# Running sums of the exponentials on two engines, pinned lane work, and value products of two key blocks in a row, in a conformer and attention layer

## The chip, the cores and the metric

The kernel runs on one core of a Trainium2 chip. Its engines are TensorE (PE in the profile, with its weight loads as PEld), VectorE (DVE), ScalarE (ACT), GpSimd (POOL) and SyncE (SP, which issues most DMAs). The metric is the device time of one execution in microseconds, the median of several runs. Before the change it is 2803.77 us, from three runs between 2798.85 and 2807.2.

## The reference, cut to what matters

One layer of a streaming encoder for a prompt of 2048 frames and, beside it, 8 sample streams of 16 new frames with 1024 cached ones each. Half of the channels go through a convolution module, half through attention with a forget bias; one output projection and a feed-forward network follow.

```python
def _conv_module(u_hist, conv_w, conv_b, ln_g, ln_b):
    y = lax.conv_general_dilated(...) + conv_b
    mu = jnp.mean(y32, axis=-1, keepdims=True)
    var = jnp.mean(jnp.square(y32 - mu), axis=-1, keepdims=True)
    y32 = (y32 - mu) * lax.rsqrt(var + EPS) * ln_g + ln_b
    return jax.nn.silu(y32)

def _attend(q, k, v, cum_q, cum_k, q_pos, k_pos):
    s = jnp.einsum('bqhd,bkhd->bhqk', q, k) * (HEAD_DIM ** -0.5)
    s = s + (cum_q[..., :, None] - cum_k[..., None, :])
    s = jnp.where(k_pos[None, :] <= q_pos[:, None], s, NEG_INF)
    p = jax.nn.softmax(s, axis=-1)
    return jnp.einsum('bhqk,bkhd->bqhd', p, v)
...
    mix = jnp.concatenate([conv_out, attn_out], axis=-1) @ w_out
    x = x + g1 * mix
    h = _rmsnorm(x, norm2_g) * (1 + sc2) + sh2
    x = x + g2 * ((silu(h @ w_gate) * (h @ w_up)) @ w_down)
```

There are 8 heads of 64 channels. The softmax divides by the sum of the exponentials, and it is these sums that the change adds up in another way.

## The kernel before

The stages follow one another: modulation and projections (to about 620 us), attention (621 to 1177), the output projection (`project_out`, from 1187), and the two halves of the feed-forward network. All of it is fp32, so that most products run in two passes and show as two records in the profile. The change touches the attention stage.

`attend` runs one of 16 steps: a pair of heads p (0 to 3) and a block of 512 queries qb (0 to 3). It goes over 4 qb + 4 key blocks of 128; the last four lie on the diagonal and are cut and masked. For each key block and head, PE makes the scores in two products (L1004 and L1010, with a mask at L1012) in one of three PSUM banks, ACT the exponential e (L1014). `values` (L971) then multiplies e with V, in tiles of 64 columns, one for each head, side by side; it is called two key blocks behind the scores. The sums of the exponentials are made on PE too, by products with ones (`add_up`, L960) in tiles of 32 columns, up to four of them side by side. For full key blocks GpSimd first adds the exponentials of two neighbouring blocks (tile `two`, L980), so that PE has 96 terms of full blocks; the blocks on the diagonal go to PE one by one (128 terms). At the end of a step the sums are stored, inverted (L1058) and read back some scores later by a list of due times, and the values divided (L1066).

Other work is woven into the steps. `score_maxima` computes an upper bound of the scores ahead of them: a product (mx, L923) in one of two banks, reduced on DVE (M, L928); it runs 32 scores and more ahead. `background` is the "lane": it holds one PSUM bank and runs five chunks of `conv_norm` (the layer norm of the convolution) and eight `sample_batch` (attention of the sample streams) one after another. Each is a generator that gives way at its `yield`s; `nback` is the number of such parts that the steps share out. Lane instructions get a later priority (`BACK_BY`) when they are issued. `behind` pins a product of the lane behind the newest score product, but most of the lane's operations on DVE, ACT and PE are not pinned, so the scheduler places them where their data is ready. A sample batch makes scores with cached keys (kc) and with its new ones (kS), adds them to a tile S, takes the maximum, the exponential, transposes S, multiplies with cached values (vc) and new ones (vn), scales the result (ob) and transposes it into catS.

`project_out` accumulates in all eight PSUM banks, and its eighth is the lane's, so its products for that bank stand behind the lane's end. Its first 63 products fill seven banks.

Of the kernel before, what the change touches and what calls it, by code (L numbers as in the profile page):

```python
# [16 lines left out]
P = 128  # L17
# [101 lines left out]
class Layer:  # L119
# [587 lines left out]
    def conv_norm(self, ch, sp, bank):  # L707
# [9 lines left out]
        def channel_mean(src):  # L717
            pm = bank
            for j in range(4):
                self.behind(nc.tensor.matmul)(pm[32 * j:32 * j + 32, :n], self.ones[:, 0:32], src[j], start=True, stop=True,  # L720
                                 tile_position=(0, 32 * j))
            m = sp.tile([P, 512], F32, tag="cm", name="cm")
            nc.scalar.copy(m[:, :n], pm[:, :n])
            po = bank
            nc.tensor.matmul(po[:, :n], self.mean, m[:, :n], start=True, stop=True)
            return po

        mu = channel_mean([y[:, j, :n] for j in range(4)])
        ms = sp.tile([P, 512], F32, tag="cw", name="cmu")
        nc.scalar.copy(ms[:, :n], mu[:, :n])  # L730
        yield
        sqs = []
        for j in range(4):
            nc.vector.tensor_tensor(y[:, j, :n], y[:, j, :n], ms[:, :n], ALU.subtract)
            sq = sp.tile([P, 512], F32, tag="cq", name="cq", bufs=4)
            nc.scalar.activation(sq[:, :n], y[:, j, :n], AF.Square)
            sqs.append(sq[:, :n])
        yield
        var = channel_mean(sqs)
        v = sp.tile([P, 512], F32, tag="cv", name="cvar")[:, :n]  # L740
        nc.vector.tensor_scalar(v, var[:, :n], EPS, None, ALU.add)
        r = sp.tile([P, 512], F32, tag="cr", name="cr")[:, :n]
        nc.scalar.activation(r, v, AF.Ln)
        nc.scalar.activation(r, r, AF.Exp, scale=-0.5)
        newton_rsqrt(nc, r, sp.tile([P, 512], F32, tag="cm", name="ct")[:, :n], v, 1)
        yield
        for j in range(4):
            z = y[:, j, :n]
            nc.vector.tensor_tensor(z, z, r, ALU.mult)
# [30 lines left out]
    def attention(self, ctx):  # L780
# [4 lines left out]
        self.waiting, self.due, self.last_s = [], [], None  # L785
# [11 lines left out]
        nback, done, units, scored = 15 + 5 * 9 + 12 + 8 * 11, 0, 0, AHEAD  # L797
# [37 lines left out]
    def first_weights(self):  # L835
# [109 lines left out]
    def attend(self, p, qb, n):  # L945
# [5 lines left out]
        z, sums = [], []  # L951

        started = set()

        def add_up(terms, last=False):
            if terms and not started:
                z.append(self.bank("tr", "sm"))
# [7 lines left out]
        def values(kt, off, es):  # L965
# [4 lines left out]
            for h in range(2):  # L970
                product = nc.tensor.matmul(z[0][HD * h:HD * h + HD, off:], V[kt // 4][:, kt % 4, HD * h:HD * h + HD], es[h][:, off:],  # L971
                                           start=(kt == 0), stop=(kt == nkt - 1), tile_position=(0, HD * h))
                if h == 0:
                    self.after(product, self.last_s)
            self.last_product = product
            if kt < 4 * qb:
                if kt % 2 == 0:
                    for h in range(2):
                        two = wk.tile([P, 512], F32, tag="two", name="two", bufs=6)
                        nc.gpsimd.tensor_tensor(two, es[h], self.waiting[0][3][h], ALU.add)  # L980
# [6 lines left out]
            if kt % 2 == 0:  # L987
                return
            if kt == nkt - 1:
                zc = wk.tile([P, 512], F32, tag="zc", name="zc")  # L990
                self.last_exp = nc.scalar.copy(zc, z[0])  # L991
            add_up(sums, kt == nkt - 1)
            sums.clear()
            if kt == nkt - 1:
                self.end_of_step(p, qb, zc, z[1])

        for kt in range(nkt):
# [4 lines left out]
            for h in range(2):  # L1002
# [10 lines left out]
                e = wk.tile([P, 512], F32, tag="e", name="e", bufs=12)  # L1013
                self.last_piece = nc.scalar.activation(e[:, off:], s[:, off:], AF.Exp)  # L1014
# [16 lines left out]
    def end_of_step(self, p, qb, zc, sums):  # L1031
# [37 lines left out]
        self.due += [(self.nscore + k, f) for k, f in ((2, load), (6, invert), (9, back), (14, divide))]  # L1069

    def behind(self, op):

        def issue(*args, **kw):
            ins = op(*args, **kw)
            self.after(ins, self.last_s)
            return ins
        return issue

    def sample_setup(self, bank):
# [27 lines left out]
        for kt in range(8):  # L1107
            self.behind(nc.tensor.matmul)(pt[:n, 2 * kt:2 * kt + 2], lf[:, kt, :], self.ones[:, 0:2], start=True, stop=True)
        suf = sm.tile([P, 8], F32, name="suf")
        nc.vector.memset(suf[:n, 7:8], 0.0)  # L1110
        for kt in range(6, -1, -1):
            nc.vector.tensor_tensor(suf[:n, kt:kt + 1], pt[:n, 2 * kt + 2:2 * kt + 3], suf[:n, kt + 1:kt + 2], ALU.add)
        yield
        for b in range(2):
            pb = bank.rearrange("p (i k) -> p i k", i=4)
            for i in range(4):
                self.behind(nc.tensor.matmul)(pb[:n, i, :], lf[:, 4 * b + i, :], tri, start=True, stop=True)
            nc.vector.tensor_tensor(
                bias[:n, b * 512:(b + 1) * 512].rearrange("p (i k) -> p i k", i=4), pb[:n],
# [7 lines left out]
        nc.tensor.matmul(pn[:n, :], lm.rearrange("p s h -> p (s h)"), sel[:, NS:], start=True, stop=True)  # L1127
# [25 lines left out]
    def sample_batch(self, b, bank):  # L1153
# [4 lines left out]
        for c in range(3):  # L1158
# [8 lines left out]
            pc = bank  # L1167
            for g in range(NP):
                self.behind(nc.tensor.matmul)(pc[32 * g:32 * g + 32, :w], self.Qbd[:, g, b].rearrange("p h q -> p (h q)"), kt[:, g, :],
                                              start=True, stop=True, tile_position=(0, 32 * g))  # L1170
# [4 lines left out]
            nc.vector.tensor_tensor(S[:, c0:c0 + w], S[:, c0:c0 + w], pc[:, :w], ALU.add)  # L1175
            if c == 2:
                nc.vector.tensor_tensor(S[:, c0:], S[:, c0:], self.maskS, ALU.add)
            yield
        nm = sm.tile([P, 1], F32, tag="nm", name="nm", bufs=2)
# [586 lines left out]
```

## Time and profile before

| | |
|---|---|
| Median of three runs | 2803.77 us |
| The profiled execution's own time | 2804.06 us |
| Its span in the profile | 2802.3 us |
| Mean granted PE clock | 0.985 |
| Attention, first score to last sum | 621.4 to 1176.4 us |
| First product of project_out | 1187.18 us |
| First product in the lane's bank | 1205.05 us |

In the profile a group of instructions is named by its line, engine and tiles, followed by its count, its busy time and the mean of one in ns, and by the idle time of its engine just ahead of it with what ended it. A busy time of PE holds everything between issue and end of its matmuls, pipeline fill included. A row of waits gives the total, the number and the longest of one. In a timeline the first column is the start in us, the second the duration of a row; neighbours of one kind share a row, with their count. PE's weight loads run beside its products.

### The profile page before, as it was taken

The page shows a single profiled execution, that of the slowest core. Times are in us where ns is not written, and L with a number is a line of the kernel's source. Part 1 is how long each engine was busy: PE and PEld are TensorE (multiplying, and loading weights), DVE is VectorE, ACT ScalarE, POOL GpSimd, SP SyncE. Part 2 cuts the span into 40 slices and gives each one's busy share as a digit, 9 for nine tenths or more (in the row PEclk, how much of TensorE's full clock was granted, in tenths as well). Part 3 has the DMA queues.
Part 4 walks back from the last instruction along what each step waited for, and adds up shares of the span by engine and source line. Part 5 has one row for each costly group of instructions (what it writes and reads, how often), then busy time and mean ns, then how long its engine had stood idle before and what let it go on. Part 6 is the DMA issues. An engine that isn't in the chain of part 4 may idle for free. (4 is left out here: it accounts for less than half of the span.)

```text
span 2802.3 us, 48143 instructions
## 1 busy us (share of the span) xinstructions
PE 2719.9 (97%) x16666; PEld 2388.6 (85%) x16666; DVE 1975.1 (70%) x3951; ACT 1237.1 (44%) x2406; POOL 461.2 (16%) x616
## 2 busy tenths in 40 slices
PE   7999999999999999999999999999999999999999
PEld 6899988864445545499999999999999999999999
DVE  2798898966465454235397989877886778766765
ACT  4443323344343444434354446444554446555552
POOL 3454411222222222214201121000000000000000
PEclk9999999989999999999999999999999999999999
DMA  9753567674426676355576869866786769788873
GB/s 328 248 192 107 189 220 265 203 199 123 124 73 192 175 233 176 116 192 187 177 265 205 305 204 314 272 217 214 240 288 208 227 194 319 245 279 262 274 252 116
DMA packets 406348, 603.49 MB, mean 215 GB/s; under 512 B 61556, under 2 KB 264468, under 8 KB 404056
## 3 DMA queue, kind: packets, MB, share of 16 engines
q1 hardware_dynamic: 405976, 600.31, 66.7%
q8 instruction: 131, 2.15, 0.3%
q14 instruction: 113, 0.93, 0.1%
q0 software_dynamic: 128, 0.11, 0.0%
HBM read 426.00 MB, written 174.25 MB: 214 GB/s over the span
## 5 line engine op out<-in xcount | busy, mean ns | idle before, releaser
L1556 PE MATMUL z<-rT,rW 128*128 128x360 f32 (+1 forms) x8316 | 1383.7, 328 | 4.5 <-ACT rW L1260 1.4
L1556 PEld LDWEIGHTS z<-rT,rW 128*128 128x128 f32 x8316 | 1379.8, 188 | 6.3 <-ACT rW L1260 2.1
L1260 ACT ACTIVATE rW<-rR 128x512 fp32r<-128x512 f32 x714 | 434.1, 616 | 382.5 <-PE z L1556 275.9
L1261 DVE TENSOR_TENSOR rW<-rR,rW 128x512 fp32r<-128x512 f32 x714 | 476.8, 673 | 149.3 <-ACT rW L1260 144.7
L702 DVE SCALAR_TENSOR_TENSOR cv<-cu,cpar,cv 128x384 f32<-128x384 f32 x580 | 311.7, 615 | 2.9 <-ACT cv L700 2.9
L928 DVE TENSOR_REDUCE M<-mx 128x1 f32<-128x512 f32 (+2 forms) x320 | 189.7, 607 | 146.5 <-PE mx L923 105.2
L1014 ACT ACTIVATE e<-s 128x512 f32<-128x512 f32 (+3 forms) x320 | 168.4, 533 | 278.2 <-PE s L1012 140.2
L514 PE MATMUL z<-hqx,wqh 128*128 128x384 f32 (+1 forms) x768 | 197.5, 333 | 0.1
L980 POOL TENSOR_TENSOR two<-e 128x512 f32<-128x512 f32 x96 | 127.2, 1342 | 398.3 <-ACT e L1014 328.0
L1260 ACT ACTIVATE rT<-traw 128x360 fp32r<-128x360 f32 (+1 forms) x315 | 149.3, 501 | 91.7 <-DMA traw<-gt_d 58.1
L1261 DVE TENSOR_TENSOR rT<-traw,rT 128x360 fp32r<-128x360 f32 (+1 forms) x315 | 157.7, 531 | 42.7 <-ACT rT L1260 42.4
L923 PEld LDWEIGHTS mx<-K,Q 96*128 96x128 f32 x320 | 63.7, 201 | 116.6 <-DVE M L928 54.7
L923 PE MATMUL mx<-K,Q 96*128 96x512 f32 (+2 forms) x320 | 145.2, 463 | 17.1 <-DVE M L928 12.6
L971 PE MATMUL pv<-e,V 128*64 128x512 f32 (+3 forms) x640 | 156.6, 565 | 3.0 <-ACT zc L991 3.0
L514 PEld LDWEIGHTS z<-hqx,wqh 128*128 128x128 f32 x768 | 136.0, 188 | 16.6 <-issue 12.4
L1484 DVE TENSOR_TENSOR rR<-rR 128x512 f32<-128x512 f32 (+1 forms) x136 | 94.2, 712 | 57.2 <-DMA rR<-w_down 52.0
L1244 PE MATMUL acc<-ch,woh 128*128 128x360 f32 (+1 forms) x384 | 128.1, 336 | 4.9 <-DVE xo L1252 2.6
L1244 PE MATMUL acc<-ch,wol 128*128 128x360 f32 (+1 forms) x384 | 128.1, 334 | 0.0
L1004 PE MATMUL s<-Q,K 128*128 128x512 f32 (+3 forms) x320 | 127.6, 399 | 0.0
L514 PE MATMUL z<-hqx,wql 128*128 128x384 f32 (+1 forms) x384 | 126.5, 329 | 0.0
L1244 PE MATMUL acc<-cl,woh 128*128 128x360 f32 (+1 forms) x384 | 122.3, 331 | 0.0
L1010 PE MATMUL s<-Q,K 128*128 128x512 f32 (+3 forms) x320 | 119.3, 373 | 0.0
(307 smaller groups left out, 3581.5 us busy)
## 6 DMA issues: line engine op xcount, KB each, us to landing
rR<-sup_d SPq DMA_DIRECT2D x176, 256.0 KB
rR<-w_gate SPq DMA_DIRECT2D x132, 256.0 KB
traw<-gt_d SPq DMA_DIRECT2D x154, 180.0 KB
rR<-w_down SPq DMA_DIRECT2D x104, 256.0 KB
rR<-sdn_d SPq DMA_DIRECT2D x96, 256.0 KB
rR<-w_up SPq DMA_DIRECT2D x88, 256.0 KB
sup_d<-rR SPq DMA_DIRECT2D x88, 256.0 KB
wa<-w_ada SPq DMA_DIRECT2D x16, 1024.0 KB
```

The costliest lines, as they stand in the source:

```text
L514: nc.tensor.matmul(z[:, :n], w[:, m], x[:, :n], start=(c == 0 and k == 0), stop=(c == CB - 1 and k == 2))
L702: self.pin(nc.vector.scalar_tensor_tensor(dst, src, w, acc[i], ALU.mult, ALU.add))
L923: self.mx.append(nc.tensor.matmul(mx[:, :w], Q2[0:AUX, h, j * P:(j + 1) * P], K2[kb][0:AUX, h, :w], start=True, stop=not diag))
L928: self.last_max = nc.vector.tensor_reduce(M[:, i, kb:kb + 1], mx[:, :w], AX.X, ALU.max)
L971: product = nc.tensor.matmul(z[0][HD * h:HD * h + HD, off:], V[kt // 4][:, kt % 4, HD * h:HD * h + HD], es[h][:, off:], start=(kt == 0), s ...
L980: nc.gpsimd.tensor_tensor(two, es[h], self.waiting[0][3][h], ALU.add)
L1004: first = nc.tensor.matmul(s[:, off:], K1[kb][:, h, sl], Q1[:, h, off:], start=True, stop=False)
L1014: self.last_piece = nc.scalar.activation(e[:, off:], s[:, off:], AF.Exp)
L1244: self.nc.tensor.matmul(z[:, :n], w[:, m], y, start=(first and i == 0 and k == 0), stop=(last and i == len(terms) - 1 and k == 2))
L1260: copy = self.nc.scalar.activation(hi, raw, AF.Copy)
L1261: engine.tensor_tensor(lo, raw, f32(hi), ALU.subtract)
L1556: nc.tensor.matmul(z, W[:, x, m], t[:, y, :w], start=(k == 0 and i == 0), stop=(k == n - 1 and i == 2))
```

## The change

Three things change in the attention stage.

- **Sums.** For the full key blocks of a step, one running sum for each head is kept in SBUF: GpSimd adds the first head's exponentials, DVE the second's, 84 adds each in all. At the diagonal the running sums are multiplied with ones together with the diagonal's terms. PE's terms of full blocks fall from 96 to 24; the 128 of the diagonal stay and are dealt out otherwise among the four tiles.
- **Values.** `values` is called for two key blocks in a row, at every odd key block, when more than three wait. The products of the second are pinned behind those of the first. There are 16 buffers for e, 12 before.
- **Lane.** All operations of the lane are pinned behind the newest operation of attention on their engine: behind the last score on PE, the last exponential on ACT, the last reduce on DVE, the last running sum on GpSimd. The lane is cut into more parts (237, not 160). The 40 subtractions and multiplications of `conv_norm` move from DVE to GpSimd. vn is loaded earlier. The due times of the division grow, and w_out's raw tiles share a ring of four buffers with the running sums.

The core of the diff:

```diff
@@ conv_norm
-            nc.vector.tensor_tensor(y[:, j, :n], y[:, j, :n], ms[:, :n], ALU.subtract)
+            self.gp(y[:, j, :n], y[:, j, :n], ms[:, :n], ALU.subtract)
+        yield
...
-            nc.vector.tensor_tensor(z, z, r, ALU.mult)
+            self.gp(z, z, r, ALU.mult)
+        yield
@@ attention
-        nback, done, units, scored = 15 + 5 * 9 + 12 + 8 * 11, 0, 0, AHEAD
+        nback, done, units, scored = 232 + 5, 0, 0, AHEAD
@@ first_weights
-                raw = self.awk.tile([P, 512], F32, tag="raw", name="raw")
+                raw = self.awk.tile([P, 512], F32, tag="acc", name="raw", bufs=4)
@@ attend
                 if h == 0:
-                    self.after(product, self.last_s)
+                    self.after(product, self.last_s if kt % 2 == 0 else self.last_product)
             self.last_product = product
-            if kt < 4 * qb:
-                if kt % 2 == 0:
-                    for h in range(2):
-                        two = wk.tile([P, 512], F32, tag="two", name="two", bufs=6)
-                        nc.gpsimd.tensor_tensor(two, es[h], self.waiting[0][3][h], ALU.add)
-                        sums.append((2 * (kt // 2 % 2) + h, 0, two))
-                elif kt % 4 == 1:
-                    ready, sums[:] = sums[:-2], sums[-2:]
-                    add_up(ready)
+            d = kt - 4 * qb
+            if d < 0:
+                if kt == 0:
+                    held.extend(es)
+                elif kt == 1:
+                    acc.extend(wk.tile([P, 512], F32, tag="acc", name="sums", bufs=4) for h in range(2))
+                if kt:
+                    self.last_add = nc.gpsimd.tensor_tensor(acc[0], es[0], acc[0] if kt > 1 else held[0], ALU.add)
+                    self.late(nc.vector.tensor_tensor, self.last_max)(acc[1], es[1], acc[1] if kt > 1 else held[1], ALU.add)
                 return
-            sums.extend((2 * (kt % 2 if qb else 0) + h, off, es[h]) for h in range(2))
...
+            if d == 0:
+                held[:] = [(h, 0, x) for h, x in enumerate(acc)]
+            part = 2 * (d % 3 == 0 if qb else 0)
+            held.extend((part + h, off, es[h]) for h in range(2))
+            if d == 3:
...
+                add_up(held, True)
                 self.end_of_step(p, qb, zc, z[1])
+            elif d == 1:
+                n = 4 if qb else 2
+                add_up(held[:n])
+                del held[:n]
...
-                e = wk.tile([P, 512], F32, tag="e", name="e", bufs=12)
+                e = wk.tile([P, 512], F32, tag="e", name="e", bufs=16)
...
-                    if len(self.waiting) > 2:
+                    if len(self.waiting) > 3 and kt % 2:
+                        self.next_values()
                         self.next_values()
@@ end_of_step
-        self.due += [(self.nscore + k, f) for k, f in ((2, load), (6, invert), (9, back), (14, divide))]
+        self.due += [(self.nscore + k, f) for k, f in ((3, load), (8, invert), (13, back), (20, divide))]
-    def behind(self, op):
+    def late(self, op, last):
 
         def issue(*args, **kw):
             ins = op(*args, **kw)
-            self.after(ins, self.last_s)
+            self.after(ins, last)
             return ins
         return issue
+    def pe(self, *args, **kw):
+        return self.late(self.nc.tensor.matmul, self.last_s)(*args, **kw)
...
+    def dve(self, name, *args, **kw):
+        return self.late(getattr(self.nc.vector, name), self.last_max)(*args, **kw)
+
+    def gp(self, *args):
+        return self.late(self.nc.gpsimd.tensor_tensor, self.last_add)(*args)
@@ sample_batch
-            nc.vector.tensor_tensor(S[:, c0:c0 + w], S[:, c0:c0 + w], pc[:, :w], ALU.add)
...
+                vn = sm.tile([QS, DC], F32, tag="vn", name="vn")
+                nc.sync.dma_start(vn, a["o_v"][T + b * QS:T + (b + 1) * QS, :])
             yield
+            self.dve("tensor_tensor", S[:, c0:c0 + w], S[:, c0:c0 + w], bank[:, :w], ALU.add)
```

How the order moves, at three places. First PE in the middle of a step of the last head pair, before: scores (s), maxima (mx), values (pv) and one lane operation (four transposes of S).

```order
L971 MATMUL pv<-e,V_7015 64x512 x2
L923 MATMUL mx<-K_6640,Q_6652 128x512
L1004 MATMUL s<-Q_10019,K_6642 128x512
L1010 MATMUL s<-Q_6635,K_6640 128x512
L923 MATMUL mx<-K_6643,Q_6652 128x512
L1004 MATMUL s<-Q_10019,K_6642 128x512
L1010 MATMUL s<-Q_6635,K_6640 128x512
L971 MATMUL pv<-e,V_7015 64x512 x2
L1189 MATMUL lane<-ident,S 128x128 x4
```

PE at the same place of the changed kernel:

```order
L1016 MATMUL s<-Q_9599,K_6642 128x512
L1022 MATMUL s<-Q_6635,K_6640 128x512
L933 MATMUL mx<-K_6640,Q_6652 128x512
L1016 MATMUL s<-Q_9599,K_6642 128x512
L1022 MATMUL s<-Q_6635,K_6640 128x512
L933 MATMUL mx<-K_6643,Q_6652 128x512
L1016 MATMUL s<-Q_9599,K_6642 128x512
L1022 MATMUL s<-Q_6635,K_6640 128x512
L980 MATMUL pv<-e,V_7015 64x512 x4
```

The values now come four at a time, for two key blocks and two heads, behind four scores, where two came behind two scores before.

Second, DVE while the lane is in its last chunk of `conv_norm`, before: reduces (M from mx), and four subtractions of the chunk in a row.

```order
L928 TENSOR_REDUCE M_1_6655<-mx_9333 128x1
L928 TENSOR_REDUCE M_1_6655<-mx_9344 128x1
L734 TENSOR_TENSOR cy_8191<-cy_8191,cmu_8232 128x128 x4
L928 TENSOR_REDUCE M_1_6655<-mx_9371 128x1
L928 TENSOR_REDUCE M_1_6655<-mx_9395 128x1
```

DVE of the changed kernel, in the same chunk (L1087 is the line of the helper `late`; `sums` is the second head's running sum, `ct` and `cr` belong to the chunk):

```order
L938 TENSOR_REDUCE M_0_6654<-mx_9299 128x1
L938 TENSOR_REDUCE M_0_6654<-mx_9316 128x1
L1087 SCALAR_TENSOR_TENSOR ct_9153<-cr_9132 128x128
L1087 TENSOR_TENSOR ct_9153<-ct_9153,cvar_9121 128x128
L1087 SCALAR_TENSOR_TENSOR cr_9132<-ct_9153,cr_9132 128x128
L938 TENSOR_REDUCE M_0_6654<-mx_9333 128x1
L1087 TENSOR_TENSOR sums_9146<-e_9260,sums_9146 128x512
L938 TENSOR_REDUCE M_0_6654<-mx_9353 128x1
L1087 TENSOR_TENSOR sums_9146<-e_9278,sums_9146 128x512
```

The four subtractions in a row are gone from DVE, and an addition stands behind a reduce, one for each full key block.

Third, PE behind the last sum, before (R spreads the inverse sums of the last step; acc is project_out's):

```order
L960 MATMUL sm<-e,ones 32x128 x2
L1074 MATMUL lane<-kc,Qbd 32x512 x2
L1043 MATMUL R<-sm,four 128x512
L1074 MATMUL lane<-kc,Qbd 32x512 x4
L1074 MATMUL lane<-kS,Qbd 32x16 x4
L1189 MATMUL lane<-ident,S 128x128 x4
L1244 MATMUL acc<-ch,woh 128x368
```

PE of the changed kernel there, and then where the lane goes on behind the 63 products of project_out that need no bank of the lane:

```order
L969 MATMUL sm<-e,ones 32x128 x2
L1087 MATMUL lane<-vc,pT 32x128 x24
L1056 MATMUL R<-sm,four 128x512
L1087 MATMUL lane<-vc,pT 32x128 x4
L1087 MATMUL lane<-vn,pTn 32x128 x4
L1087 MATMUL lane<-ident,ob 128x128
L1087 MATMUL lane<-kc,Qbd 32x512 x8
L1280 MATMUL acc<-ch,woh 128x368
```

```order
L1280 MATMUL acc<-cl,woh 128x368
L1087 MATMUL lane<-kS,Qbd 32x16 x4
L1087 MATMUL lane<-ident,S 128x128 x8
L1087 MATMUL lane<-ident,S 16x128
L1087 MATMUL lane<-vc,pT 32x128 x32
L1087 MATMUL lane<-vn,pTn 32x128 x4
L1087 MATMUL lane<-ident,ob 128x128
L1087 MATMUL lane<-kc,Qbd 32x512 x8
L1087 MATMUL lane<-kS,Qbd 32x16 x4
L1087 MATMUL lane<-ident,S 128x128 x8
L1087 MATMUL lane<-ident,S 16x128
L1087 MATMUL lane<-vc,pT 32x128 x32
```

Before, the last batch of the sample streams was half done on PE when project_out began; in the changed order the rest of the last but one and the whole last batch stand behind project_out's first 63 products.

More of the change, by code (lines that the diff above doesn't have):

```diff
@@ L717, in channel_mean @@
         def channel_mean(src):
-            pm = bank
             for j in range(4):
-                self.behind(nc.tensor.matmul)(pm[32 * j:32 * j + 32, :n], self.ones[:, 0:32], src[j], start=True, stop=True,
-                                 tile_position=(0, 32 * j))
+                self.pe(bank[32 * j:32 * j + 32, :n], self.ones[:, 0:32], src[j], start=True, stop=True, tile_position=(0, 32 * j))
+            yield
             m = sp.tile([P, 512], F32, tag="cm", name="cm")
[L723 to L728, printed above, removed]
+            self.copy(m[:, :n], bank[:, :n])
+            yield
+            self.pe(bank[:, :n], self.mean, m[:, :n], start=True, stop=True)
+            yield
+        yield from channel_mean([y[:, j, :n] for j in range(4)])
         ms = sp.tile([P, 512], F32, tag="cw", name="cmu")
-        nc.scalar.copy(ms[:, :n], mu[:, :n])
+        self.copy(ms[:, :n], bank[:, :n])
         yield
@@ L733, in conv_norm @@
         for j in range(4):
[L734 removed]
+            self.gp(y[:, j, :n], y[:, j, :n], ms[:, :n], ALU.subtract)
+        yield
+        for j in range(4):
             sq = sp.tile([P, 512], F32, tag="cq", name="cq", bufs=4)
[L736 removed]
+            self.act(sq[:, :n], y[:, j, :n], AF.Square)
             sqs.append(sq[:, :n])
+            yield
         yield
[L739 removed]
+        yield from channel_mean(sqs)
         v = sp.tile([P, 512], F32, tag="cv", name="cvar")[:, :n]
[L741 removed]
+        self.dve("tensor_scalar", v, bank[:, :n], EPS, None, ALU.add)
+        yield
         r = sp.tile([P, 512], F32, tag="cr", name="cr")[:, :n]
[L743 to L745 removed]
+        self.act(r, v, AF.Ln)
+        self.act(r, r, AF.Exp, scale=-0.5)
+        yield
+        t = sp.tile([P, 512], F32, tag="cm", name="ct")[:, :n]
+        self.dve("scalar_tensor_tensor", t, r, -0.5, r, ALU.mult, ALU.mult)
+        yield
+        self.dve("tensor_tensor", t, t, v, ALU.mult)
+        yield
+        self.dve("scalar_tensor_tensor", r, t, 1.5, r, ALU.add, ALU.mult)
         yield
@@ L950, in attend @@
         nkt = 4 * qb + 4
-        z, sums = [], []
-        started = set()
+        z, held, acc, started = [], [], [], set()
         def add_up(terms, last=False):
-            if terms and not started:
+            if not started:
                 z.append(self.bank("tr", "sm"))
@@ L1107, in sample_setup @@
         for kt in range(8):
-            self.behind(nc.tensor.matmul)(pt[:n, 2 * kt:2 * kt + 2], lf[:, kt, :], self.ones[:, 0:2], start=True, stop=True)
+            self.pe(pt[:n, 2 * kt:2 * kt + 2], lf[:, kt, :], self.ones[:, 0:2], start=True, stop=True)
+        yield
         suf = sm.tile([P, 8], F32, name="suf")
@@ L1166, in sample_batch @@
                 kt = kS
-            pc = bank
             for g in range(NP):
-                self.behind(nc.tensor.matmul)(pc[32 * g:32 * g + 32, :w], self.Qbd[:, g, b].rearrange("p h q -> p (h q)"), kt[:, g, :],
-                                              start=True, stop=True, tile_position=(0, 32 * g))
+                self.pe(bank[32 * g:32 * g + 32, :w], self.Qbd[:, g, b].rearrange("p h q -> p (h q)"), kt[:, g, :],
+                        start=True, stop=True, tile_position=(0, 32 * g))
             if c < 2:
```

63 lines of the change are left out of this document (33 added, 30 removed).

## The prediction

> **What bounds the kernel now.** I read the page first, then the busy times by stretch, then the groups of the attention stretch, then the timeline of TensorE (PE).
>
> ```profile
> span 2802.3 us, 48143 instructions
> PE 2719.9 (97%) x16666; PEld 2388.6 (85%) x16666; DVE 1975.1 (70%) x3951; ACT 1237.1 (44%) x2406; POOL 461.2 (16%) x616
> ...
> core 0: us, PE busy (x) PEld busy (x) DVE busy (x) ACT busy (x) POOL busy (x), PEclk, DMA share, GB/s
> 620.00:1178.00 558.00, 537.06 (x3160) 269.97 (x3159) 277.92 (x512) 228.60 (x448) 133.22 (x104) 0.97 0.51 151
> ```
>
> PE is busy for 97% of the span. The change touches the attention stretch (scores from 621 us, last sum of exponentials at 1176) and the few steps behind it. There PE is busy for 537 of 558 us, so about 21 us is all that a better order can win back from PE's waits; anything beyond must come from PE doing less, or doing it more densely. DVE (VectorE) is at 50%, POOL (GpSimd) at 24%: there is room for adds on both, on average.
>
> Now the waits of PE in that stretch, and what two stages look like on PE at close range: score products and maxima (full 128-column tiles), then value products in tiles of 64 columns, then sums in tiles of 32.
>
> ```profile
> engine line waited for: us in total, times, longest us
> PE mx L923 <- DVE M L928: 9.7, 9, 3.2
> PE pv L971 <- ACT zc L991: 3.0, 1, 3.0
> PE mx L923 <- DVE suf L1112: 2.8, 1, 2.8
> PE lane L1074 <- DMA cy<-y_d: 2.3, 1, 2.3
> PE lane L1074 <- DVE S L1175: 2.1, 1, 2.1
> ```
> ```profile
> 999.48 1.08 PE L971 MATMUL pv<-e,V 128*64 128x512 f32 x4
> 1000.49 0.50 PE L923 MATMUL mx<-K,Q 96*128 96x512 f32 x1
> 1000.83 0.39 PE L1004 MATMUL s<-Q,K 128*128 128x512 f32 x1
> ...
> 1014.79 0.40 PE L1004 MATMUL s<-Q,K 128*128 128x512 f32 x1
> 1015.02 0.40 PE L1010 MATMUL s<-Q,K 128*128 128x512 f32 x1
> 1015.35 1.08 PE L971 MATMUL pv<-e,V 128*64 128x512 f32 x4
> ...
> 1172.62 1.06 PE L960 MATMUL sm<-two,ones 128*32 128x512 f32 x8
> 1173.50 1.03 PE L960 MATMUL sm<-e,ones 128*32 128x512 f32 x8
> ```
>
> The first column is the start. Between full tiles the next matmul starts 0.23 us later (1014.79 to 1015.02). From a full tile to a narrow one it takes 0.33 (1015.02 to 1015.35): 0.10 more. A group of narrow tiles runs at 0.88 per two passes of 512 columns (1172.62 to 1173.50), but the group of values that stands alone takes 1.01 until a full tile follows (999.48 to 1000.49): 0.13 more; and that full tile then takes 0.34 until its successor (to 1000.83): 0.10 more. So **each visit of PE to narrow tiles costs about 0.32 us** beside its work, and no wait shows it: it is inside "busy".
>
> **The change, part by part.** Sums are against the profiled execution, 2804.06 us (span 2802.3 and 1.8 around it), which lies 0.3 us over the median of the three runs.
>
> (1) Visits to narrow tiles. I counted them in the order of PE from the first score to the last sum: 197 stretches of narrow tiles before, 146 after. Stretches with value products fall from 160 to about 80, since products of two key blocks follow one another; stretches of lane work alone grow from 35 to 56, as the lane is cut finer. 51 visits x 0.32 = **-16.3 us**.
>
> (2) Sums of exponentials on PE. The running sums replace, in each step with qb full blocks of four, qb passes of four 512-column terms by one: (0+1+2) x 4 head pairs = 12 passes x 0.88 = 10.6. The diagonal's terms are dealt out anew, 128 columns less in each of 12 steps: 0.88/4 x 12 = 2.6. Together **-13.2 us**, all on PE and so on the path.
>
> (3) Lane work that now falls behind the attention on PE. In the order 60 products with vc, 10 with kc, 8 transposes of S and 2 of ob are no longer ahead of the last sum. By the rows below, 32 products with vc (64 records, two passes) take 1.96, four with kc one group of 0.88 like the sums, four transposes 0.60, one of ob 0.33: 60/32 x 1.96 + 10/4 x 0.88 + 2 x 0.60 + 2 x 0.33 = 3.7 + 2.2 + 1.2 + 0.7 = 7.8, **-7.8 us** in the attention; it comes back in (4).
>
> (4) The tail. These rows are PE's between the last sum and the first product of project_out's eighth accumulator, whose bank the lane holds.
>
> ```profile
> 1176.40 0.63 PE L960 MATMUL sm<-e,ones 128*32 128x256 f32 x8
> ...
> 1182.86 0.26 PE L1074 MATMUL lane<-kS,Qbd 128*32 128x16 f32 x8 [3.00 <-DVE S L1175]
> 1186.30 1.11 PE L1189 MATMUL lane<-ident,S 128*128 128x128 f32 x4 [3.19 <-ACT S L1182]
> 1187.18 0.68 PE L1244 MATMUL acc<-ch,woh 128*128 128x368 f32 x1
> ...
> 1190.90 0.60 PE L1189 MATMUL lane<-ident,S 128*128 128x128 f32 x4
> ...
> 1199.58 0.27 PE L1195 MATMUL lane<-ident,S 128*16 128x128 f32 x1
> 1201.24 1.96 PE L1207 MATMUL lane<-vc,pT 128*32 128x128 f32 x64 [1.40 <-ACT pTn L1197]
> ...
> 1204.08 0.33 PE L1214 MATMUL lane<-ident,ob 128*128 128x128 f32 x1 [0.54 <-DVE ob L1211]
> 1205.05 0.41 PE L1244 MATMUL acc<-ch,woh 128*128 128x368 f32 x1 [0.64 <-DVE catS L1217]
> ```
>
> Before, the lane ends 1205.05 - 1176.40 = 28.7 us behind the last sum: one sample batch, most of it hidden behind the first 63 products of project_out (1187.2 to 1199.6, 12.4 us). In the changed order the end of the last batch but two (vc, ob) and the kc products of the last but one stand ahead of those 63 products, the rest of the last but one and the whole last batch behind them, one link after another in one bank. The first product of project_out waits for sm, R, the reciprocal and a store and load of cat as before: 1187.18 - 1176.40 = 10.8, which hides what stands ahead. Then 12 for the 63. The rest of a batch from kS on: 1182.86 to 1187.4 is 4.5 to the end of its first transposes, 1.4 for the second ones and their copy, 5.5 from 1199.58 to 1205.05: 11.4. A whole batch adds two rounds of kc and the add to S, 3.4: 14.8. 10.8 + 12 + 11.4 + 14.8 = 49.0, against 28.7: **+20.3 us**. Bounds: +28 with loads that come 8 us late (third rival); +9 if the rest of the last batch but one hides behind the 63 products as one batch did before.
>
> (5) Waits of PE: what goes and what comes. These are the bursts on DVE, and what adds cost there:
>
> ```profile
> 792.25 4.62 DVE L749 TENSOR_TENSOR cy<-cy,cr 128x512 f32<-128x512 f32 x4
> ...
> 797.53 0.79 PE L923 MATMUL mx<-K,Q 96*128 96x512 f32 x1 [3.16 <-DVE M L928]
> ```
> ```profile
> L734 DVE TENSOR_TENSOR cy<-cy,cmu x20: 279/686/1779, 669.2 to 858.1; 128x512 f32<-128x512 f32 x16, 128x128 f32<-128x128 f32 x4
> L749 DVE TENSOR_TENSOR cy<-cy,cr x20: 281/679/1778, 686.1 to 871.2; 128x512 f32<-128x512 f32 x16, 128x128 f32<-128x128 f32 x4
> L980 POOL TENSOR_TENSOR two<-e x96: 1256/1281/1836, 638.6 to 1164.8; 128x512 f32<-128x512 f32 x96
> ```
> ```profile
> L928 DVE TENSOR_REDUCE M<-mx 128x1 f32<-128x512 f32 (+3 forms) x290 | 173.8, 612 | 144.7 <-PE mx L923 103.6 <-PE mx L927 39.2
> L1014 ACT ACTIVATE e<-s 128x512 f32<-128x512 f32 (+3 forms) x320 | 168.4, 533 | 278.2 <-PE s L1012 140.2 <-PE s L1010 132.8 <-POOL two L980 0.2
> ...
> L734 DVE TENSOR_TENSOR cy<-cy,cmu 128x512 f32<-128x512 f32 (+1 forms) x20 | 19.4, 1029 | 0.0
> L749 DVE TENSOR_TENSOR cy<-cy,cr 128x512 f32<-128x512 f32 (+1 forms) x20 | 15.1, 815 | 0.0
> ```
>
> Four of conv_norm's multiplies in a row hold up the reduces for 4.6 us, and the maxima on PE for 3.2. Those 40 operations go to POOL, and every lane operation now stands behind the newest reduce, score or exponential on its engine. Of the 20 us of waits quoted I take 10 as gone: the bursts (most of the 9.7). The others need a chain or a DMA to be shorter, which a later place may or may not give.
>
> New are 84 adds on DVE among the reduces, and 84 on POOL in place of 96. POOL's are 1.28 us each, as before, and its 40 more from conv_norm make 84 x 1.28 + 40 x 1.28 = 159 us in 558: no bound. A DVE add with two inputs in SBUF and the same shape took 0.68 us, and up to 1.78 where POOL ran an add at the same time; the step was 1.10, most of a POOL add. Two of them go with each pair of full key blocks (42 pairs), among four reduces. The maxima have two banks, so the fourth maximum of the pair, about 2.4 us behind the first (three times 0.24 for a maximum and 0.47 for a score), needs the second reduce: 0.24 + 2 x 0.61 + one add of 0.68 to 1.78 = 2.1 to 3.2 us. The wait is 0 to 0.9 a pair; with POOL adding for about 1.3 of each 3.3 us some four in ten meet it: 0.35 x 42 = 15. The ends are 0 and 42 x 0.9 = 38. Net **+5 us** (-20 with all old waits gone and no new one, +38 with the reverse).
>
> The page "SBUF — State Buffer" of the Trainium skill (section "🔬 SBUF: two separate sides") speaks against splitting the heads between these two engines: it says that such a DVE operation and a GpSimd one that reads SBUF take their shared ports as a lock, and the loser waits for the whole instruction. The largest durations of L734 and L749 (1.78) agree with it; by the page alone every overlap would cost that much, which is the first rival below.
>
> At no cost I put: 16 buffers for e instead of 12, since the exponentials waited for POOL to free one for 0.2 us in all, beside 279 us that ScalarE waited for scores; the later due times of the division, since nothing before project_out reads these columns; the earlier load of vn; and the tiles of w_out that now share a ring with the running sums, whose next user is project_out too. If that cover goes, a load that PE waits for costs what the one in the waits did, 2.3 us, or in the tail what the third rival says.
>
> Sum: 2804.1 - 16.3 - 13.2 - 7.8 + 20.3 + 5 = 2792.1; **forecast 2792 us**, 0.4% faster.
>
> **Rivals.** *DVE becomes the bound through the shared add* (slower). A pair of key blocks has PE busy for 537.06/80 = 6.7 us now and (537.06 - 37.3)/80 = 6.25 after, a mean over full and diagonal pairs. DVE needs 4 x 0.61 for reduces, 2 adds, and for the rest (277.92 - 173.8 - 19.4 - 15.1)/80 = 0.87: 3.3 + 2 adds. It passes PE where an add takes over 1.47 us on average. At 1.78 it is 6.9, 0.63 too much: 42 x 0.63 = +26, so 2818. For it: POOL and DVE are released by the same exponentials, so their adds start together. Against: the two streams then run out of step, and the median of L734 among POOL's adds was 0.69, near its shortest at that shape.
>
> *The pins free PE wholly* (faster): all of the 20 us of waits quoted go, and the adds find gaps: 2804.1 - 37.3 + 20.3 - 20 = 2767. For it: the waits are nine bursts and four single events, all in the lane. Against: two banks for maxima.
>
> *The tail eats it* (no change): the last two batches run with no cover, and their loads (1 MB tiles, four of them) collide with w_out and cat. The stretch moves 151 GB/s, so 1 MB is 7 us; one such tile too late is about +8: 2800. For it: two buffers each for kc and vc; against: nothing else wants the DMAs for 12 us.
>
> **How the numbers follow.** Forecast 0.45 (2782 to 2800), DVE bound 0.20 (2812 to 2826), pins 0.15 (2759 to 2777), tail 0.20 (2796 to 2808). Our measurement tells about 0.3%, 8.4 us, from no change: faster is under 2795.4. The forecast's range lies four fifths under that: 0.36; with the pins 0.51. Same: 0.09 of the forecast, 0.18 of the tail: 0.27. Slower: 0.20 of DVE bound, 0.02 of the tail: 0.22. The range leaves half of the pins' case (0.07) and the upper quarter of DVE bound (0.05) out: 2768 to 2821.
>
> **What would show it.** In the changed profile: narrow visits at 0.32 and about 146 of them (1); sums from full blocks in 24 terms in place of 96 (2) and a shorter stretch from 621 to the last sum, by 30 us less the waits; the lane's end 49 us behind that sum (4); adds of L1087 on DVE at 0.7 with a tail to 1.8, and PE's waits for M at 10 to 25 us (5). The prediction is wrong if the DVE adds average over 1.4 us, if PE waits for M over 40 us, or if the lane's end lies under 35 or over 60 us behind the last sum.

## The result, and the profile after

The changed kernel takes 2823.11 us, median of 4 runs (2819.84 to 2828.96), against 2802.4 (2798.85 to 2807.2) before: 1.0075 times as long, interval 1.0051 to 1.0099. It is slower, where 2792 and a gain were forecast, and 2 us above the range. The profiled execution is the longest of the four, 2828.96 us.

The page of the changed kernel, and its busy times by stretch (first score to last sum of exponentials, then to the first product in project_out's eighth bank):

```profile
span 2827.2 us, 47974 instructions
PE 2720.6 (96%) x16522; PEld 2403.8 (85%) x16522; DVE 2005.4 (71%) x3995; ACT 1237.0 (44%) x2406; POOL 489.6 (17%) x644
...
core 0: us, PE busy (x) PEld busy (x) DVE busy (x) ACT busy (x) POOL busy (x), PEclk, DMA share, GB/s
619.30:1164.90 545.60, 515.85 (x2837) 274.31 (x2838) 299.82 (x542) 225.08 (x441) 163.33 (x132) 0.95 0.49 143
1164.90:1223.10 58.20, 37.30 (x346) 25.68 (x339) 18.91 (x34) 16.70 (x27) 0.00 (x0) 0.71 0.51 173
```

The same two stretches of the kernel before:

```profile
621.40:1176.40 555.00, 534.12 (x3145) 268.57 (x3144) 276.36 (x509) 227.16 (x445) 133.22 (x104) 0.97 0.52 152
1176.40:1205.00 28.60, 19.84 (x177) 15.97 (x175) 14.71 (x22) 15.66 (x24) 0.00 (x0) 0.88 0.40 130
```

The 24.9 us of span come out as -9.4 in the attention, +29.6 in the tail, -2.1 ahead of the first score and +6.8 behind the tail. The attention lost 18 us of PE's busy time, not 37, and got 9 us more of waiting. The granted clock (the number behind the busy time of POOL) fell from 0.97 to 0.95 there, and from 0.88 to 0.71 in the tail.

PE's waits in the attention, and the groups of the new adds and of the sums. A row of waits gives total, number and longest; a group ends with its idle time:

```profile
PE mx L933 <- DVE M L938: 12.8, 19, 1.5
PE lane L1087 <- DMA cy<-y_d: 5.1, 2, 2.9
PE lane L1087 <- DVE S L1087: 4.9, 4, 2.9
```
```profile
L992 POOL TENSOR_TENSOR sums<-e,sums 128x512 f32<-128x512 f32 x72 | 95.3, 1324 | 98.0 <-ACT e L1026 96.3
L1087 DVE TENSOR_TENSOR sums<-e,sums 128x512 f32<-128x512 f32 x72 | 61.8, 858 | 2.9 <-ACT e L1026 2.2
L969 PE MATMUL sm<-sums,ones 128*32 128x512 f32 x48 | 28.2, 719 | 0.6 <-DVE sums L1087 0.5
L1087 DVE TENSOR_TENSOR sums<-e 128x512 f32<-128x512 f32 x12 | 8.7, 726 | 7.5 <-ACT e L1026 7.5
```

The waits for the reduces (M) are more, and shorter: 19 instead of 9. DVE's 84 adds take (61.8 + 8.7)/84 = 0.84 us on average. And 48 records of the running sums have 28.2 us of busy time on PE, more than 192 of the pairs had before (26.4). Busy time counts overlap with other products too; what the sums cost from record to record follows further down.

The timeline of PE in the tail, with the idle time ahead of a row and its releaser; one row is ScalarE's:

```profile
1171.22 0.47 PE L1087 MATMUL lane<-ident,ob 128*128 128x128 f32 x1 [2.91 <-DVE ob L1087]
1172.24 1.94 PE L1087 MATMUL lane<-kc,Qbd 128*32 128x512 f32 x8 [0.55 <-DVE catS L1087]
...
1177.88 0.67 PE L1280 MATMUL acc<-ch,woh 128*128 128x368 f32 x1 [0.95 <-ACT ch L1296]
...
1191.22 0.26 PE L1087 MATMUL lane<-kS,Qbd 128*32 128x16 f32 x8
...
1194.14 1.28 ACT L1087 ACT_TABLE_LOAD   x1
...
1196.74 1.12 PE L1087 MATMUL lane<-ident,S 128*128 128x128 f32 x4 [5.26 <-ACT S L1087]
...
1201.05 3.38 PE L1087 MATMUL lane<-vc,pT 128*32 128x128 f32 x64 [0.34 <-ACT pTn L1087]
...
1206.19 1.07 PE L1087 MATMUL lane<-kc,Qbd 128*32 128x512 f32 x8 [0.55 <-DVE catS L1087]
...
1213.26 1.11 PE L1087 MATMUL lane<-ident,S 128*128 128x128 f32 x4 [3.06 <-ACT S L1087]
...
1217.68 3.59 PE L1087 MATMUL lane<-vc,pT 128*32 128x128 f32 x64 [0.34 <-ACT pTn L1087]
...
1223.13 0.41 PE L1280 MATMUL acc<-ch,woh 128*128 128x368 f32 x1 [0.64 <-DVE catS L1087]
```

Two batches stand there uncovered, link after link, as the order said. But the same 64 records with vc take 3.4 to 3.6 us where they took 1.96 before: PE is busy for only 37 of the 58 us, and the granted clock during these two rows is 0.55 and 0.53, where it was 1.00 before.

### The profile page after: what moved, and what is told of

The parts are those of the page before. It is cut to its first block, busy times and chain, and to the rows that moved or that the text cites. A ratio compares the mean times of both kernels' runs of the same rounds, so it can differ in the third digit from the quotient of the medians.

```text
span 2827.2 us, 47974 instructions
## 1 busy us (share of the span) xinstructions
PE 2720.6 (96%) x16522; PEld 2403.8 (85%) x16522; DVE 2005.4 (71%) x3995; ACT 1237.0 (44%) x2406; POOL 489.6 (17%) x644
## 4 chain that ended last, share of the span: by engine, by line
PE 50%; DMA 3%; DVE 2%; issue 1%; ACT 0%; SPq 0%; POOL 0%; DVEq 0%; ACTq 0%; POOLq 0%
PE z L1592 46%; PE acc L1280 4%; DMA rR<-w_up 1%; DVE rR L1520 0%; DMA traw<-ht_d 0%; DMA cr<-cat_d 0%; DVE rW L1297 0%; DMA ht_d<-ot 0%; PE pr L1389 0%; POOL nx L1405 0%; DMA rR<-w_gate 0%; DVE cl L1297 0%; DMA x_d<-xo 0%; DMA ht_d<-xo 0%; ACT rW L1296 0%
## 5 line engine op out<-in xcount | busy, mean ns | idle before, releaser
L933 PE MATMUL mx<-K,Q 96*128 96x512 f32 (+2 forms) x320 | 142.9, 464 | 16.9 <-DVE M L938 15.1
L980 PE MATMUL pv<-e,V 128*64 128x512 f32 (+3 forms) x640 | 138.1, 551 | 0.0
L1016 PE MATMUL s<-Q,K 128*128 128x512 f32 (+3 forms) x320 | 132.1, 413 | 1.9 <-ACT e L1026 1.9
L1022 PE MATMUL s<-Q,K 128*128 128x512 f32 (+3 forms) x320 | 121.0, 378 | 0.0
L992 POOL TENSOR_TENSOR sums<-e,sums 128x512 f32<-128x512 f32 x72 | 95.3, 1324 | 98.0 <-ACT e L1026 96.3
```

Source lines behind the costliest of these rows:

```text
L933: self.mx.append(nc.tensor.matmul(mx[:, :w], Q2[0:AUX, h, j * P:(j + 1) * P], K2[kb][0:AUX, h, :w], start=True, stop=not diag))
L1016: first = nc.tensor.matmul(s[:, off:], K1[kb][:, h, sl], Q1[:, h, off:], start=True, stop=False)
L1022: self.last_s = nc.tensor.matmul(s[:, off:], K2[kb][:, h, sl], Q2[:, h, off:], start=False, stop=not diag)
```

## Experiments

The first two take the tail apart from the attention. Theory T1 is that the lane is dealt out too late; T2, that the loss is in the attention. The loop over STEPS deals the lane's parts out by `nback`, along 320 scores. The kernel before has some 130 parts and counts 160 (the 160 that "The change" gives is this count), so that its last part is dealt out before score 240; the changed kernel has some 237 and counts 237, and deals the last between scores 264 and 288.

**e1_pace**

```diff
-        nback, done, units, scored = 232 + 5, 0, 0, AHEAD
+        nback, done, units, scored = 320, 0, 0, AHEAD
```

> The changed kernel with one number changed: the lane's parts are shared out as if there were 320 of them instead of 237, so that on TensorE only one product with vc and its end are left behind the last sum, as in the kernel before. Theory T1 (the lane is dealt out too late; two batches run without cover, and TensorE's clock is halved there): the stretch from the last sum to project_out's eighth bank falls from 58 us to 25 to 32, and the time from 2823 to 2793 to 2802 us, if the attention gets 3 to 6 us longer by the lane work that it takes back. Theory T2 (the attention itself is slower by adds that contend): the stretch gets shorter but the attention longer by as much, and the time stays over 2810 us.

2793.38 us, 0.9974 of the kernel before (0.9962 to 0.9985): 30 us less than the change, by one number.

```profile
622.00:1164.40 542.40, 512.66 (x3016) 275.79 (x3015) 305.92 (x557) 228.59 (x445) 164.94 (x132) 0.97 0.53 156
1164.40:1191.30 26.90, 20.47 (x160) 16.37 (x159) 13.24 (x19) 16.00 (x24) 0.00 (x0) 0.81 0.44 137
```

The tail falls from 58.2 to 26.9 us, and the attention, which takes the lane's work back, gets no longer: 542.4, where 3 to 6 us more were expected. T1 holds.

**e2_before_late**, the reverse on the kernel before:

```diff
-        nback, done, units, scored = 15 + 5 * 9 + 12 + 8 * 11, 0, 0, AHEAD
+        nback, done, units, scored = 133, 0, 0, AHEAD
```

> The kernel before with one number changed: the lane's parts are shared out as if there were 133 of them instead of 160, so that a whole sample batch and most of another are left behind the attention, as in the changed kernel; nothing else of the change is in it. T1: the stretch from the last sum to project_out's eighth bank grows from 28.7 us to 50 to 60, and the time by 15 to 25 us to about 2820. T2: the late lane is hidden or is paid for by a shorter attention, and the time stays within 6 us of 2802.

2825.10 us, 1.0088 (1.0072 to 1.0103), 22 us more; nothing of the change is in it.

```profile
616.80:1173.70 556.90, 535.13 (x3034) 265.99 (x3033) 271.13 (x501) 225.33 (x440) 134.90 (x104) 0.98 0.48 143
1173.70:1223.50 49.80, 31.74 (x286) 22.77 (x285) 18.70 (x32) 19.36 (x30) 0.00 (x0) 0.73 0.47 160
```

The tail grows by 21 us, and the clock in it falls from 0.88 to 0.73. So the lane's pace is enough for a slowdown of this size. What is left: e1 gains 9 us, where visits and sums were to save 29.5 and new waits to cost 5. Of the others, e5, e9, e4, e3 and e6 start from e1, and e7, e8 and e10 from e5.

**e5_pace_gp_sums**

```diff
-                    self.late(nc.vector.tensor_tensor, self.last_max)(acc[1], es[1], ...)
+                    self.last_add = nc.gpsimd.tensor_tensor(acc[1], es[1], ...)
```

> e1 with the second head's running sums on GpSimd too, so that VectorE has none of the 84 adds, and GpSimd 168. If the adds on VectorE are what TensorE's waits for the reduces in the attention come from (15 us in 24 waits, with half clock after the long ones), those waits fall under 6 us and the attention is 10 to 25 us shorter than in e1. If the waits come from the lane's operations on VectorE, they stay over 10 us, and the attention is within 5 us of e1. GpSimd would be busy for about 168 x 1.3 + 40 x 1.2 = 270 us of 545, no bound.

2774.45 us, 0.9895 (0.9874 to 0.9916), 19 us less than e1.

```profile
618.60:1135.50 516.90, 486.78 (x2933) 269.32 (x2934) 250.74 (x467) 229.94 (x446) 263.56 (x216) 0.98 0.54 160
1135.50:1170.40 34.90, 25.99 (x248) 18.43 (x240) 15.27 (x25) 13.83 (x22) 0.00 (x0) 0.79 0.52 167
```
PE's waits for M, and for a load into Q, in e1 and then in e5:

```profile
PE mx L933 <- DVE M L938: 16.4, 26, 2.2
...
PE s L1022 <- DMA Q<-mrow: 2.1, 2, 1.8
```
```profile
PE mx L933 <- DVE M L938: 10.0, 14, 2.3
PE s L1022 <- DMA Q<-mrow: 8.1, 4, 5.2
```

The attention is 25.5 us shorter than e1's, of which the tail gives 8 back, as more of the lane is left. GpSimd is busy for 264 of 517 us, and no wait of PE is for it. The waits for M fall from 16.4 to 10.0, less than expected; but those for the load grow as the others shrink, and PE's waits in all stay where they were (29.7 us in e1, 30.1 in e5). So the gain lies wholly in PE's busy time, which falls by 26 us. From the start of one record to the next, the sums take 8.9 us less, the lane 6.1, as more of it is left for the tail, and scores and maxima 11. Of this 11, half clock explains up to 3; the fewer visits to narrow tiles (126 in place of 144) explain some 4, an estimate with the 0.24 us a visit that e7 and e8 give; the rest stays open.

What became of the sums is seen in the order. In e1 the first head's term goes ahead alone, three maxima in a row behind it, and the others follow later. The rows of PE's order, e1 first, then e5:

```
L980 MATMUL pv<-e,V_7013 64x384 x2
L969 MATMUL sm<-sums,ones 32x512
L933 MATMUL mx<-K_6628,Q_6652 128x512
L933 MATMUL mx<-K_6633,Q_6652 128x512
L933 MATMUL mx<-K_6640,Q_6652 128x512
...
L969 MATMUL sm<-sums,ones 32x512
L969 MATMUL sm<-e,ones 32x512 x2

L980 MATMUL pv<-e,V_7013 64x384 x2
L969 MATMUL sm<-sums,ones 32x512 x2
L969 MATMUL sm<-e,ones 32x512 x2
```

A pass of four terms is torn into one and three. Ten of the twelve passes are torn in e1 and none in e5, and the sums take 8.9 us more from record to record, 0.9 for each torn pass: it costs twice. The running sums' records have 25.4 us of busy time in e1 and 13.3 in e5:

```profile
L969 PE MATMUL sm<-sums,ones 128*32 128x512 f32 x48 | 25.4, 656 | 1.2 <-DVE sums L1087 1.1
```
```profile
L969 PE MATMUL sm<-sums,ones 128*32 128x512 f32 x48 | 13.3, 636 | 0.0
```

**e9_together** keeps the four together and leaves the adds on VectorE:

```diff
+                if i == 0:
+                    lead = self.last_product
+                else:
+                    self.after(self.last_product, lead)
...
-                held[:] = [(h, 0, x) for h, x in enumerate(acc)]
+                held[:] = [(h, 0, x) for h, x in enumerate(acc)][::-1]
```

> e1 with the four terms of the running sums' pass kept together on TensorE: the second head's term first and the others ordered behind it. In e1 22 rows of the order hold terms of the running sums, since the first head's often go ahead alone; here 12. If terms that go ahead alone cost a pass of their own (0.9 us each, the stretch of the sums 46 us against 38 in e5), the sums' time on TensorE falls by 7 to 9 us and the attention by as much. If TensorE then waits for VectorE's last add instead, waits for the sums rise by as much as the sums' own time falls, and the attention stays within 3 us of e1.

2794.33 us, 0.9967 (0.9955 to 0.9979): as e1.

```profile
L969 PE MATMUL sm<-sums,ones 128*32 128x512 f32 x48 | 17.7, 827 | 1.6 <-DVE sums L1091 1.4
...
618.60:1166.40 547.80, 518.89 (x3016) 278.71 (x3015) 305.51 (x557) 227.14 (x445) 164.90 (x132) 0.95 0.52 154
```

The running sums' busy time falls by 8 us, as expected, but the attention is 5 us longer than e1's, and PE's waits for the sums hardly move (1.4 us, 1.1 in e1): neither branch of the expectation. The clock is 0.95 where e1 had 0.97, which is 12 us more lost at half clock, and PE's waits for the reduces are 17.9 us. With the adds still on VectorE, curing the tearing alone gains nothing here.

**e4_pace_old_sums** goes back to the sums of the kernel before (`two` on GpSimd, 96 terms of full blocks), with 14 buffers for e.

```diff
+                        two = wk.tile([P, 512], F32, tag="two", name="two", bufs=6)
+                        self.last_add = nc.gpsimd.tensor_tensor(two, es[h], self.waiting[0][3][h], ALU.add)
...
-                    self.late(nc.vector.tensor_tensor, self.last_max)(acc[1], es[1], ...)
```

> e1 with the sums of the kernel before (pairs added on GpSimd, 96 terms of full blocks on TensorE; the exponentials have 14 buffers instead of 16): no adds on VectorE. Visits 115 in the order for 144, terms of the sums 224 for 152, a whole batch more behind the attention. If the running sums as split here gain nothing, because VectorE's part costs waits, half clock and torn passes (25 us between e1 and e5), the attention is within 5 us of e1 or shorter. If they are worth the 13 us that fewer passes save, it is 10 us longer or more.

2782.76 us, 0.9933 (0.9909 to 0.9957), 11 us less than e1.

```profile
619.50:1136.00 516.50, 491.77 (x3037) 270.01 (x3038) 236.44 (x459) 225.18 (x440) 171.73 (x144) 0.98 0.51 152
```

With 72 more terms of sums on PE than e5 (11.6 us more from record to record) and no add on VectorE, the attention is as short as e5's (the tail is 45.5 us, with a batch more in it). So the running sums, split in this way, cost more than the passes they save.

**e3_pace_no_pair** takes the value products of each key block by themselves again.

```diff
-                    if len(self.waiting) > 3 and kt % 2:
-                        self.next_values()
+                    if len(self.waiting) > 2:
                         self.next_values()
```

> e1 with the value products of each key block issued by themselves again, two key blocks behind the scores; 205 visits of TensorE to narrow tiles between first score and last sum in the order in place of 144. If a visit costs 0.32 us beside its work, the attention is 20 us longer than in e1, and more of the lane is left behind it (one whole batch more): 15 to 30 us over e1 in all. If the visits are hidden by waits, it is within 6 us of e1 in the attention.

2794.66 us, 0.9974 (0.9964 to 0.9985): as e1. The waits for M are halved (7.5 us in 13, against 16.4 in 26), and the attention is 536.6 us, 6 shorter; the tail, with more of the lane, is 7 longer:

```profile
617.60:1154.20 536.60, 518.95 (x2918) 258.56 (x2919) 308.71 (x551) 228.07 (x443) 163.68 (x132) 0.98 0.52 154
```

PE is busier by 6 us and waits 12 less. Is a visit free, then? **e7_gp_350** is e5 with `nback` at 350, and **e8_gp_no_pair** undoes the pairs in it, as in e3.

> e5 with the lane's parts shared out as if there were 350 of them, not 320, so that about 32 products with vc fewer are left behind the last sum on TensorE. The stretch from there to project_out's eighth bank falls from 35 us to 28 to 32, the attention stays within 4 us of 517: 2766 to 2772 us. If the lane's earlier parts only wait in the attention, the attention grows by as much and the time stays at 2774.

> e7 with the value products of each key block issued by themselves again: 189 visits of TensorE to narrow tiles in the order in place of 118, and 32 products with vc more left behind the attention. VectorE has no adds here. If a visit's 0.32 us is a cost of its own wherever VectorE does not hold TensorE back, the attention is 18 to 24 us longer than in e7 and the time 2775 to 2788 us. If it is bought back by shorter waits as in e3, the attention is within 6 us of e7.

e7: 2758.67 us, 0.9844 (0.9824 to 0.9863). e8: 2779.55 us, 0.9909 (0.9879 to 0.9938). Their attentions, e7 first:

```profile
618.90:1128.20 509.30, 484.63 (x2991) 269.68 (x2989) 247.87 (x468) 227.16 (x445) 264.87 (x216) 0.98 0.54 162
```
```profile
619.40:1139.80 520.40, 501.66 (x2918) 257.30 (x2919) 252.53 (x467) 229.29 (x443) 265.34 (x216) 0.98 0.53 159
```

71 more visits make PE busier by 17 us, 0.24 a visit, with about 2 us less of vc in it; 6 us come back as shorter waits, so the attention grows by 11, between the two branches that were expected. The tail, with more of the lane, adds 8. In time the pairs are worth 21 us where VectorE has no adds, and nothing where it has; in the attention alone they save 11 and cost 6. e7 beats both kernels; of its 16 us under e5, 8 are in the attention, which had not been expected.

**e6_pace_no_pins** drops the lane's pins on ScalarE, VectorE and GpSimd and those of its transposes on PE; one of the five changes:

```diff
-        return self.late(getattr(self.nc.vector, name), self.last_max)(*args, **kw)
+        return getattr(self.nc.vector, name)(*args, **kw)
```

> e1 with the lane's operations unpinned on ScalarE, VectorE and GpSimd, and its transposes on TensorE; products stay behind the newest score. If the pins are what keeps bursts of the lane away from the reduces, waits of the maxima for them rise from 16 us to over 25 and the attention by 10 us or more. If they do nothing, both stay within 5 us of e1.

2794.29 us, 0.9979 (0.9966 to 0.9992): as e1, with 14.9 us of waits for M and 545.5 us of attention (542.4 in e1). The pins do nothing that these runs can tell.

**e10_cy_dve** is e7 with conv_norm's 40 operations on VectorE (`self.dve("tensor_tensor", ...)` for `self.gp(...)`).

> e7 with the 40 subtractions and multiplications of conv_norm on VectorE again, pinned behind the newest reduce. If the move to GpSimd is what keeps TensorE's waits for the reduces low, they rise from 7 us to 13 or more (each burst of four held the maxima for 1.6 to 3.2 us in the kernel before) and the time from 2759 to 2766 to 2775 us. If GpSimd, with 168 adds, was the later place for them, the time falls or stays within 4 us.

2765.78 us, 0.9881 (0.9842 to 0.9919). The waits for M are 9.0 us, 2 more than e7's, where 6 more were expected. The median lies 7 us over e7's, but the intervals overlap; and the attention, 521.3 us, is 12 longer with 8 us more of the lane's work in it, so that the two orders differ in more than the place of these operations. At best the move is a small gain, and this is not settled.

## Why the prediction was wrong

The profile's span grew by 24.9 us where the sum has -12.0: 37 us apart. Of these, 23 lie in the attention, 9 in the tail and 5 outside both. In the table, the attention's terms are taken from the start of one record of PE to the start of the next, waits apart, and the visits are what is left:

| Term | Forecast, us | Measured, us |
|---|---|---|
| (1) visits | -16.3 | -6.6 |
| (2) sums | -13.2 | -4.2 |
| (3) lane work | -7.8 | -7.4 |
| (5) waits | +5 | +8.8 |
| (4) tail | +20.3 | +29.6 |
| ahead of the attention and behind the tail | 0 | +4.7 |

So three steps failed, by 9 us or so each: the sums were priced as if no pass were torn, the visits were added to the waits as if the two were independent and the clock stayed, and the tail was priced from rows at full clock and with shorter waits. Without the late tail the forecast of a gain would have held in sign (e1). That e1's 2793 us lies on the forecast is chance: for a lane dealt out in time the same sum gives 2804.1 - 16.3 - 13.2 + 5 = 2780.

- **The tail (4)** had the right mechanism and sign, and the wrong size. By its stages: 13.0 us to project_out's first product (10.8 in the sum), 13.3 for its 63 products (12), 15.0 for the rest of a batch (11.4) and 16.9 for the whole one (14.8). The two groups of vc took 3.4 and 3.6 us at half clock instead of 1.96, together 3 us more. And PE waited 5.3 us for the first exponential of S, not 3.2: the exponential now comes behind operations of project_out, a SiLU (L1336) and splits of w_out, and in the trace a table load of 1.28 us stands ahead of it on ScalarE, which is not there before. e1 and e2 show that the tail alone decides the sign. That it comes from `nback`, a count that had paced the lane well only because it was larger than the number of parts, stood in the code and wasn't seen; 237 is about the true number.
- **The waits (5)**: +5 forecast, +9 measured (20.9 to 29.7 us between PE's records). That is near; what failed is that a wait was priced at its length alone. A slip in the working hides some of it: three times 0.24 and 0.47 is 2.1 us and not 2.4, so that a pair waits up to 1.1 us, and the term would have been about +8. This stretch of the changed kernel shows what a wait costs beyond its length:

```profile
853.58 0.77 PE L933 MATMUL mx<-K,Q 96*128 96x512 f32 x2 [1.53 <-DVE M L938]
...
854.93 0.62 PE L969 MATMUL sm<-sums,ones 128*32 128x512 f32 x1 [0.52 <-DVE sums L1087]
...
856.94 0.63 PE L1016 MATMUL s<-Q,K 128*128 128x512 f32 x1
857.36 0.63 PE L1022 MATMUL s<-Q,K 128*128 128x512 f32 x1
```

  After 2 us of waiting within 3, score products start 0.43 us apart, not 0.23, for some 3 us: the granted clock is 0.50 from 855.87 to 859.28. Half clock begins 11 times in this attention and 7 times in that of before, and by the granted clock (0.97 and 0.95 over 555 and 546 us) some 10 us more were lost to it than before. The page "TensorE: Matmul & The Clock Gate" of the Trainium skill (section "🔬 Part 1: The HAM clock gate") has the halving, in windows of about 3.4 us, and puts it after at least one idle window. The trace agrees on the length, but not on the idle window: in the 3.4 us ahead of these 11 halvings PE was idle for 0.6 to 2.9 us, never for all of it.
- **Sums (2)**: -13.2 forecast. Their time on PE, from record to record, fell by 4 us, from 52.9 to 48.7. The passes were torn: 24 rows of the order hold terms of the running sums, where 12 passes were counted. In e5, with no add on VectorE, there are 12 such rows and the sums take 37.6, a fall of 15. The torn rows stood in the order before the run.
- **Visits (1)**: 0.32 us was a fair price of PE's busy time (0.24 between e7 and e8). The count was right too: the trace has 146 visits, before 196. In e1, where the clock is that of before, the visits give -12 by the same reckoning as in the table; in the changed kernel some 10 us of half clock lie over them. With VectorE's adds in the way, taking the pairs back costs nothing, since PE then waits 12 us less (e3); without the adds a good part of the gain stays (e7, e8). The forecast added this term to the waits as if they were independent.
- **Lane work (3)**: -7.8 forecast, -7.4 measured on PE (70.0 to 62.6 us).
- **The rivals.** DVE as the bound has 2818 and so comes near by chance of number: its mechanism needed adds of over 1.47 us on average, and they took 0.84; DVE is busy for 55% of the attention. Pins that free PE did not come (e6). The tail was the rival that came nearest in place, but it was given 8 us over the forecast and took 9 over a term that was +20 already.
- **The signs.** None of those that the prediction names for being wrong appeared: the adds took 0.84 us (limit 1.4), PE waited for M for 14.5 us (limit 40), and the lane ended 58 us behind the last sum (limit 60). No sign watched the torn passes or the clock. In the chances, "the upper quarter of DVE bound" above 2821 is more than a third of 2812 to 2826.
- The 6.8 us behind the tail stay open: the same work takes 1604 us in this profile, 1597 in that of before and 1598 to 1603 in those of e1 to e8, and no run here was made for it.

## What to carry to other kernels

Where a count paces background work, changing how finely that work is cut changes the pace: look in the new order for what is left behind the stage, and price a chain without cover at the clock that its own waits leave. Terms that are to share one pass are best made where they are ready together: here the half of the running sums on VectorE, though busy for only 55% of the time, tore the passes and stood among the reduces that free the banks of the maxima, and GpSimd, slower but waited for by no product, was the better place for both halves. After such a change look at the waits in all, since those for a load grew as the others shrank. And a denser order on the bounding engine pays only as far as those who free its banks keep up.

## What was not expected of the hardware

- GpSimd as the place of all 168 adds, at 1.3 us each, shows in no wait of PE (e5), and with 84 of them on VectorE, at 0.87 us each, the kernel takes 19 us longer (e1).
- The ports that the two share explain little of the loss. In the changed kernel 22 of the 84 adds took over 0.75 us, each of them while GpSimd was at work, which makes 13 us of VectorE's time in all; of the 14.5 us that PE waited for reduces, 2.8 us came just behind an add that was drawn out beyond 0.9 us, and 3.6 behind a shorter one. This row gives shortest, median and longest:

```profile
L1087 DVE TENSOR_TENSOR sums<-e,sums x72: 665/684/1758, 659.4 to 1153.4; 128x512 f32<-128x512 f32 x72
```

  The longest is as the page "SBUF — State Buffer" of the Trainium skill (section "🔬 SBUF: two separate sides") has it for an add that finds the ports taken; by the median, most did not, and 58 of the other 62 ran beside GpSimd for less than 0.1 us.
